# Attention scores with 128 rows in two passes instead of 64 rows in three

## The chip, the cores and the metric

The kernel runs on one core of a Trainium2 chip. The metric is the device time of one execution in microseconds (us). The core has a matrix engine (TensorE, PE in the rows), VectorE (DVE), ScalarE (ACT), GpSimd (POOL) and SyncE (SP), which issues most of the DMA transfers. Matmuls read from the on-chip buffer and write to eight accumulator banks (PSUM), each of 128 partitions by 512 float32 values.

## The reference

Two layers of a transformer block work on 512 image tokens and 256 context tokens of width 1024. Each layer has an adaLN modulation (shift, scale and gate from a 1024 x 6144 matrix), a projection of the tokens, a mixer, an output projection and a SwiGLU. The mixer has three parts: a bidirectional mLSTM of four heads, differential attention of four heads, and grouped-query attention with four query heads over two key heads. The last layer computes no context outputs. What matters here are the attention scores, all with head width 64:

```
p1 = softmax(q1 k1^T / 8),  p2 = softmax(q2 k2^T / 8)     (differential head)
out = (p1 - lam * p2) v
p  = softmax(q k^T / 8),  out = p v                         (grouped-query head)
```

Image queries see all 768 keys, context queries (layer 0 only) the 256 context keys.

## The kernel before, in words

Every float32 product is made from high and low parts. A number is split into a high part, rounded to the matmul type float32r, and the remainder, and a product a b is taken as ah bh + ah bl + al bh (`mm3`). All weights and activations are split this way; for the scores the queries and keys are.

A layer's `mixer` runs in two merged stages. The first holds the mLSTM beside the projections of the output gate, the grouped-query keys, values and queries and the first value heads. The second merges four streams (`merge`, line 354): attention (`att_gqa`, then `att_diff` for heads 0 to 3), the remaining projections (`proj`: queries and keys `b_qk(0)`, `b_qk(1)`, `b_qk(2)`, values, `b_qk(3)`), in layer 0 sixteen steps of the adaLN product (`ada_part`), and the first part of the output projection (`out_first`). `merge` gives the next piece to the stream that is least far by the costs it yields. A planner then orders the instructions of each engine by its own timeline and by these priorities; a tile can be written when one of its pool's buffers (`bufs`) is free.

`b_qk(h)` (line 729) multiplies six token tiles with the weights of a head's queries and keys, rotates them (`do_rope`, line 682), and transposes them on TensorE (`to_feat`, line 719) so that features lie on partitions: the pair's first head on partitions 0 to 63, the second on 64 to 127. `split` (line 413) writes the high part on ScalarE and the low part on VectorE. `b_qk(h)` waits for the scores of an earlier head (`need qkd`) since it takes over its buffers. `b_gkv` and `b_gq` (lines 776 and 794) do the same for the grouped-query heads, with `norm_rope`.

`softmax` (line 813) makes the scores of 128 queries for one or two heads. For each block of 512 keys, and then the remaining 256, it issues three matmuls per head, each with 64 rows of the array:

```
for x, y in ((0, 0), (0, 1), (1, 0)):
    for s, (m, QA, KA, su) in zip(ss, ops):
        hs = slice(64 * m, 64 * m + 64)
        last_qk[key] = mm(s[:, ks], QA[x][hs, qs], KA[y][hs, ks], ...)
```

The result lies in one of two score buffers of two banks each. VectorE takes its minimum (the queries carry a factor of -1/8), ScalarE the exponential with the sum. For four query tiles together, the probabilities are then transposed key block by key block (`transpose_split`), split again (tiles `ph`, `pl`) and multiplied by the values.

The adaLN steps (`ada_part`, line 160) load 128 rows of weights in two transfers of 1024 columns into three buffers (`araw`) and run four matmuls of 512 columns, side by side in four groups of 32 array columns, into the bank `acc`. This is also the only bank for the projections of the second stage. Plain float32 matmuls take two passes, so a step has eight matmul records.

The output projection in `out_first`, `first` and `second` adds to residual tiles `R`; in layer 1 these are first scaled with layer-norm rows (`pgb`) on GpSimd.

Of the kernel before, what the change touches and what calls it, by code (L numbers as in the profile page):

```python
# [12 lines left out]
F32 = mybir.dt.float32  # L13
# [35 lines left out]
def kernel(ctx: ExitStack, tc: tile.TileContext, a: dict, out: bass.AP):  # L49
# [110 lines left out]
    def ada_part(l, sc, ps, ap, tag):  # L160
# [5 lines left out]
        for k in range(KD):  # L166
            raws = []
            for i in range(2):
                raw = ap.tile([P, 1024], F32, tag="araw", name="araw", bufs=3)
                c0 = sc * 2048 + i * 1024  # L170
                nc.sync.dma_start(raw, a["w_ada"][l, k * P:(k + 1) * P, c0:c0 + 1024])
                raws.append(raw)
            pa = ps.tile([P, 512], F32, tag=tag, name="pa")
            for j in range(4):
                TE.matmul(pa[32 * j:32 * j + 32, :], cT[:, k, :], raws[j // 2][:, (j % 2) * 512:(j % 2) * 512 + 512],  # L175
                          start=True, stop=True, tile_position=(0, 32 * j))
            V.tensor_tensor(mod, mod, pa, ALU.add)
            yield 0.9
# [202 lines left out]
    def mixer(l, xh, xl, yd, ps, fill, pre):  # L381
# [300 lines left out]
        def do_rope(dst, src, T, nh):  # L682
# [10 lines left out]
            if dst.ndim == 4:  # L693
                t1, t2 = [t.rearrange("p (v j) d -> p v j d", j=2) for t in (t1, t2)]
            V.tensor_tensor(dst, t1, t2, ALU.add)

        def norm_rope(dst, src, T, nh, gi):
# [8 lines left out]
            if T >= 2:  # L706
                do_rope(dst, t, T, nh)
            else:
                V.tensor_copy(dst, t.rearrange("p (v j) d -> p v j d", j=2) if dst.ndim == 4 else t)

        nqk = 10 if last else 8

        def qk_tile(nm):
            return qkv.tile([P, NTOK], F32R, tag="qk", name=nm, bufs=nqk)
# [4 lines left out]
        def to_feat(rqs, o, dst, ts, after=None, mul=None):  # L719
            pt = ps.tile([P, 512], F32, tag="q", name="ptq")  # L720
            with tc.issue_after(last_qk[after].ins) if after in last_qk else nullcontext():
                for i, rq in enumerate(rqs):
                    TE.transpose(pt[:, i * P:(i + 1) * P], rq[:, o:o + 2].rearrange("p n d -> p (n d)"), ident)
            dh, dl, src = dst[0][:, ts], dst[1][:, ts], pt[:, 0:len(rqs) * P]
            split(dh, dl, src, mul)
# [3 lines left out]
        def b_qk(h, after):  # L729
            def go():  # L730
                wh, wl = wload([cold(C_DQ + h * P, P), cold(C_DK + h * P, P)])
                QA, KA = [qk_tile("QA") for i in range(2)], [qk_tile("KA") for i in range(2)]
                QK[h] = (QA, KA)
                for t0, t1 in ((0, 2), (2, 6)):
# [3 lines left out]
                    for T in range(t0, t1):  # L738
                        po = ps.tile([P, 512], F32, tag="acc", name="po")
                        gemm_b(po[:, c0:256], T, wh, wl, c0, 256 - c0, xh, xl)  # L740
                        rq = qkv.tile([P, 4, HD], F32, tag="rq", name="rq", bufs=4)
                        src = po[:, 0:256].rearrange("p (n d) -> p n d", d=HD)
                        if T >= 2:
                            px = qkv.tile([P, 4, HD], F32, tag="px", name="px", bufs=2)
                            S.copy(px, src)
                            do_rope(rq, px, T, 4)
                        else:
                            S.copy(rq[:, c0 // HD:], src[:, c0 // HD:])
                        rqs.append(rq)
                        yield 2.6  # L750
                    ts = slice(t0 * P, t1 * P)
                    if after is not None:
                        yield ("need", ("qkd", after))
                    if needq:
                        to_feat(rqs, 0, QA, ts, after, -0.125)
                    to_feat(rqs, 2, KA, ts, after)
                    yield 0.3 * (t1 - t0)
# [18 lines left out]
        def b_gkv():  # L776
            wh, wl = wload([cold(C_GK, 256)])
            KG, VG = [qk_tile("KG") for i in range(2)], [v_tile("VG") for j in range(2)]
            for t0, t1 in ((0, 2), (2, 6)):
                rqs = []  # L780
                for T in range(t0, t1):
# [3 lines left out]
                    norm_rope(rq[:, 0:2], po[:, 0:P].rearrange("p (n d) -> p n d", d=HD), T, 2, 1)  # L785
# [4 lines left out]
                to_feat(rqs, 0, KG, slice(t0 * P, t1 * P))  # L790
# [3 lines left out]
        def b_gq():  # L794
            wh, wl = wload([cold(C_GQ, 256)])
            QG = [[qk_tile("QG") for i in range(2)] for j in range(2)]
            for t0, t1 in qgroups:
# [9 lines left out]
                for j in range(2):  # L807
                    to_feat(rqs, 2 * j, QG[j], slice(t0 * P, t1 * P), None, -0.125)
# [4 lines left out]
        def softmax(at, key, T, ops, nk):  # L813
            qs, ss, es = slice(T * P, (T + 1) * P), [], []
# [15 lines left out]
        def hl_tiles(at, n):  # L830
            return [at.tile([P, 512], F32R, tag=t, name=t, bufs=3)[:, 0:n] for t in ("ph", "pl")]
# [12 lines left out]
        def att_diff(at, h):  # L844
            yield ("need", ("qk", h))
            QA, KA = QK[h]
            for t0, t1 in qgroups:
# [26 lines left out]
                sq = at.tile([P, 512], F32, tag="og", name="sq", bufs=3)  # L874
# [3 lines left out]
                else:  # L878
                    ov = at.tile([P, 512], F32, tag="og", name="ov", bufs=3)
# [22 lines left out]
        def att_gqa(at):  # L902
            yield ("need", ("qk", "g"))
            QG, KG, VG = QK["gq"], QK["gk"], VV["g"]
            for t0, t1 in qgroups:
                nk = CTX if t0 == 0 else NTOK
                n = (t1 - t0) * P
                for m in range(2):
                    oG = []
                    for j in range(2):  # L910
# [19 lines left out]
                        og = at.tile([P, 512], F32, tag="og", name="og", bufs=3)  # L930
# [38 lines left out]
        ps.alias = {"q": ("t",)}  # L969
        at = pool("at", bufs=2)  # L970
# [10 lines left out]
        def proj():  # L981
            yield from chain(b_qk(0, None if nqk > 8 else "g"), b_qk(1, "g"), b_qk(2, 0), b_v(2), b_qk(3, 1))
# [6 lines left out]
        def out_first():  # L989
# [15 lines left out]
            for c in range(4):  # L1005
                cs = slice(c * 256, (c + 1) * 256)
                wh, wl = wload([w_out[:, cs]])
                for i in range(2):
                    tg = ("qk", "va")[c % 2]
                    R[c, i] = qkv.tile([P, 3, 256], F32, tag=tg, name="rs", bufs={"qk": nqk, "va": 6}[tg])  # L1010
# [44 lines left out]
        w5 = [[at.tile([P, 512], F32R, tag=t, name="w5", bufs=3) for _ in range(2)] for t in ("ph", "pl")]  # L1055
# [38 lines left out]
        def third(T):  # L1094
            s, g = 1 if T < 2 else 0, T // 2
            if g not in xh:
# [5 lines left out]
                       lambda: at.tile([P, 4, P], F32, tag="og", name="v", bufs=3))  # L1102

        gb1 = [qkv.tile([P, 3, 256], F32, tag="qk", name="gb1", bufs=nqk) for _ in range(3)]
# [52 lines left out]
        at.release()  # L1157
        qkv.release()
# [325 lines left out]
```

## Time and profile before

| | |
|---|---|
| time, median of 3 runs | 2094.97 us (2090.12 to 2097.2) |
| profiled execution, time | 2088.73 us |
| its span, first to last instruction | 2086.8 us |
| TensorE busy | 1957.7 us, 94% |
| VectorE busy | 1132.7 us, 54% |
| ScalarE busy | 748.6 us, 36% |
| GpSimd busy | 332.7 us, 16% |
| mean granted TensorE clock | 0.963 |

Durations of matmuls contain the time until their results are written, so that the records of consecutive matmuls overlap: what one costs in a row of many is the distance between starts. "Busy" is the time covered by at least one record. A timeline row merges neighbours with the same line and tiles, and names the shape of the first; `64*128 64x512` is a stationary tile of 64 rows by 128 columns and a moving tile of 64 rows by 512 columns.

### The profile page before, as it was taken

The numbers are of one execution on the slowest core, as the hardware profiler recorded it, in microseconds if no ns is written. First come the engines' busy times: TensorE is split into PE (matmuls) and PEld (weight loads), VectorE is DVE, ScalarE is ACT, GpSimd is POOL, SyncE is SP. The second block draws the span as 40 slices with busy tenths as digits, with TensorE's granted clock in tenths as the row PEclk, the third lists the DMA queues.
The fourth block names the chain that finished last, engine by engine and source line by source line (L and its number), as shares of the span: only waits on it lengthen the run. The fifth ranks groups of instructions, "written<-read, shape, count | busy, mean of one in ns | idle before, by whom it ended". The sixth has DMA issues, their size and how long they took to land.

```text
span 2086.8 us, 33736 instructions
## 1 busy us (share of the span) xinstructions
PE 1957.7 (94%) x13720; PEld 1753.0 (84%) x13720; DVE 1132.7 (54%) x2247; ACT 748.6 (36%) x1457; POOL 332.7 (16%) x283
## 2 busy tenths in 40 slices
PE   7889899999889999999999988879999889999998
PEld 5778768778879999999987788878888879999886
DVE  3556555666575963532347465845665564232346
ACT  4334364444363111111234333445544352222330
POOL 1224200104316000000000011321016431000000
PEclk9998899999999999999999999989998989999999
DMA  8211261328223772532244521111116215323231
GB/s 289 62 44 36 66 185 38 97 84 226 89 72 102 225 224 63 184 104 62 83 132 149 164 91 31 45 52 41 38 34 173 80 52 172 101 86 98 89 114 61
DMA packets 207221, 215.91 MB, mean 103 GB/s; under 512 B 13584, under 2 KB 181410, under 8 KB 207066
## 3 DMA queue, kind: packets, MB, share of 16 engines
q1 hardware_dynamic: 198778, 205.63, 31.7%
q0 software_dynamic: 8288, 8.13, 1.7%
q8 instruction: 108, 1.77, 0.4%
q14 instruction: 47, 0.39, 0.1%
HBM read 196.12 MB, written 17.60 MB: 102 GB/s over the span
## 4 chain that ended last, share of the span: by engine, by line
PE 80%; DVE 9%; ACT 4%; DMA 3%; issue 2%; POOL 1%; SPq 0%; DVEq 0%; ACTq 0%; POOLq 0%
PE po L63 17%; PE pacc L63 13%; PE pg L63 12%; PE pu L63 12%; PE pc L63 6%; PE s L63 5%; PE pw L63 4%; PE pv L63 3%; PE ppt L837 2%; DVE ca L453 2%; PE pa L175 1%; DMA araw<-w_ada 1%; DVE ru L691 1%; ACT v L271 1%; PE pN L604 1%
## 5 line engine op out<-in xcount | busy, mean ns | idle before, releaser
L63 PE MATMUL po<-wh,xh 128*128 128x256 f32 (+1 forms) x832 | 250.5, 301 | 11.0 <-DVE VG L416 3.5
L63 PE MATMUL po<-wh,xl 128*128 128x256 f32 (+1 forms) x832 | 242.9, 292 | 0.0
L63 PE MATMUL po<-wl,xh 128*128 128x256 f32 (+1 forms) x832 | 242.4, 291 | 0.0
L292 POOL TENSOR_TENSOR wl<-raw,wh 128x1024 fp32r<-128x1024 f32 x56 | 135.9, 2447 | 413.8 <-ACT wh L291 336.9
L291 ACT CAST wh<-raw 128x1024 fp32r<-128x1024 f32 x142 | 142.5, 1048 | 161.7 <-PE pu L63 98.8
L63 PE MATMUL pg<-xh,wh 128*128 128x256 f32 x672 | 190.5, 283 | 1.2 <-ACT v L271 1.2
L63 PE MATMUL pg<-xh,wl 128*128 128x256 f32 x672 | 190.3, 283 | 0.0
L63 PE MATMUL pu<-xh,wh 128*128 128x256 f32 x672 | 190.2, 283 | 0.0
L63 PE MATMUL pu<-xl,wh 128*128 128x256 f32 x672 | 190.2, 283 | 0.0
L63 PE MATMUL pg<-xl,wh 128*128 128x256 f32 x672 | 190.2, 283 | 0.0
L63 PE MATMUL pu<-xh,wl 128*128 128x256 f32 x672 | 190.0, 283 | 0.0
L63 PEld LDWEIGHTS po<-wh,xh 128*128 128x128 f32 x832 | 166.2, 200 | 21.6 <-issue 6.9
L63 PE MATMUL pacc<-wl,hh 128*128 128x512 f32 x440 | 174.2, 396 | 1.0 <-DVE wl L305 1.0
L63 PE MATMUL pacc<-wh,hh 128*128 128x512 f32 x440 | 171.9, 397 | 0.6 <-ACT hh L1293 0.5
L345 POOL TENSOR_TENSOR rstd<-rstd,nhalf 128x4 f32<-128x4 f32 (+2 forms) x52 | 42.9, 830 | 788.1 <-DVE rstd L342 736.5
L63 PEld LDWEIGHTS po<-wl,xh 128*128 128x128 f32 x832 | 166.2, 200 | 1.2 <-issue 0.2
L63 PEld LDWEIGHTS po<-wh,xl 128*128 128x128 f32 x832 | 165.6, 199 | 1.1 <-issue 0.5
L63 PE MATMUL pacc<-wh,hl 128*128 128x512 f32 x440 | 162.5, 397 | 0.0
L1255 DVE SCALAR_TENSOR_TENSOR th<-th,pg 128x512 f32<-128x512 f32 x44 | 30.1, 686 | 208.4 <-ACT th L1254 208.3
L63 PEld LDWEIGHTS pg<-xh,wh 128*128 128x128 f32 x672 | 129.0, 192 | 2.2 <-ACT v L271 1.4
L1254 ACT ACTIVATE th<-pg 128x512 f32<-128x512 f32 x44 | 26.2, 598 | 290.9 <-PE pg L63 279.5
L63 PEld LDWEIGHTS pg<-xh,wl 128*128 128x128 f32 x672 | 129.0, 192 | 0.8 <-issue 0.8
(366 smaller groups left out, 5034.2 us busy)
## 6 DMA issues: line engine op xcount, KB each, us to landing
raw<-w_ffn_in SPq DMA_DIRECT2D x176, 256.0 KB
araw<-w_ada SPq DMA_DIRECT2D x80, 512.0 KB
raw<-w_ffn_out SPq DMA_DIRECT2D x66, 512.0 KB
raw<-w_in SPq DMA_DIRECT2D x32, 512.0 KB
raw<-w_out SPq DMA_DIRECT2D x18, 512.0 KB
araw<-w_ada SPq DMA_DIRECT2D x32, 256.0 KB
raw<-w_in SPq DMA_DIRECT2D x32, 256.0 KB
xr<-x1d SPq DMA_DIRECT2D x10, 512.0 KB
```

The costliest lines, as they stand in the source:

```text
L63: return TE.matmul(out, lhsT, rhs, start=start, stop=stop)
L175: TE.matmul(pa[32 * j:32 * j + 32, :], cT[:, k, :], raws[j // 2][:, (j % 2) * 512:(j % 2) * 512 + 512], start=True, stop=True, tile_positi ...
L271: S.activation(v[:, k], x, AF.Identity, scale=col[:, 0, kk:kk + 1], bias=col[:, 1, kk:kk + 1])
L291: S.copy(h, raw[:, :, 0:n])
L292: wsub[0].tensor_tensor(wl[:, 4 * hf:4 * hf + 4, 0:n], raw[:, :, 0:n], f32(h), op=ALU.subtract)
L345: last_pow[0] = G.tensor_tensor(r, r, nhalf[:, 0:n], op=ALU.pow)
L453: V.scalar_tensor_tensor(ca[:, b0:b0 + n], cr[:, b0 + t:b0 + t + n], cw[:, l, fi, t:t + 1], ca[:, b0:b0 + n], ALU.mult, ALU.add)
L604: TE.matmul(nv[:, j, d, pr], ws[d][:, j, pr], vtok[:, c, 2 * pr + j], start=d + pr == 0, stop=False, skip_group_check=True)
L691: V.tensor_tensor(t2v[:, :, :, bb], sv[:, :, :, 1 - bb], sinb[:, :, bb].unsqueeze(1).to_broadcast([P, nh, 2, 16]), ALU.mult)
L837: TE.transpose(pt[:, i * P:(i + 1) * P], e[:, kt * P:(kt + 1) * P], ident)
L1254: S.activation(th[:, 0:n], gp, AF.Tanh, scale=0.5)
L1255: V.scalar_tensor_tensor(th[:, 0:n], th[:, 0:n], 1.0, gp, ALU.add, ALU.mult)
```

## The change

The queries of one head become one tile of 128 partitions: high part on 64 partitions, low part on the other 64 (`feat_q`). The keys of one head become two tiles of 128 partitions: the high part written on both halves, and the low part on both halves (`feat_k`). A matmul of the query tile with the first key tile gives qh kh + ql kh, with the second qh kl + ql kl. Two matmuls per key block replace three, and the small term ql kl is added. To have keys on both halves, the rotated keys are written twice next to each other (`twice`) and each head of a pair is transposed by itself.

More key tiles need more room: a new pool (`more["pool"]`) holds those of the even heads, and the query tiles of layer 1 shrink to the image tokens. To make room, the tiles `ph`, `pl` and `og` go from three buffers to two, `pgb` from two to one, and the adaLN weights are loaded in four transfers of 512 columns into three buffers of half the size.

```diff
 ada_part:
-            for i in range(2):
-                raw = ap.tile([P, 1024], F32, tag="araw", name="araw", bufs=3)
-                c0 = sc * 2048 + i * 1024
-                nc.sync.dma_start(raw, a["w_ada"][l, k * P:(k + 1) * P, c0:c0 + 1024])
+            for i in range(4):
+                raw = ap.tile([P, 512], F32, tag="araw", name="araw", bufs=3)
+                c0 = sc * 2048 + i * 512
+                nc.sync.dma_start(raw, a["w_ada"][l, k * P:(k + 1) * P, c0:c0 + 512])
...
 do_rope:
-            V.tensor_tensor(dst, t1, t2, ALU.add)
+            for d, n in dst if isinstance(dst, tuple) else ((dst, 0),):
+                u1, u2 = t1[:, n:n + 2], t2[:, n:n + 2]
...
+                elif d.ndim == 4:
+                    u1, u2 = [u.unsqueeze(2).to_broadcast([P, 2, 2, HD]) for u in (u1, u2)]
+                V.tensor_tensor(d, u1, u2, ALU.add)
...
-        nqk = 10 if last else 8
-        def qk_tile(nm):
-            return qkv.tile([P, NTOK], F32R, tag="qk", name=nm, bufs=nqk)
+        def k_tiles(nm, h=1):
+            p = qkv if h % 2 else more["pool"]
+            return [[p.tile([P, NTOK], F32R, tag="qk", name=nm, bufs=4) for _ in range(2)] for _ in range(2)]
+        def q_tiles(nm, h=1):
+            p, n = (qkv, 4) if h % 2 or not last else (more["pool"], 2)
+            return [p.tile([P, NTOK - q0], F32R, tag="qq", name=nm, bufs=n) for _ in range(2)]
...
+        def feat_q(rqs, o, dst, t0, after=None):
+            src = to_feat(rqs, lambda rq: rq[:, o:o + 2].rearrange("p n d -> p (n d)"), after)
+            ts = slice(t0 * P - q0, t0 * P - q0 + len(rqs) * P)
+            for m in range(2):
+                hi, lo = slice(64 * m, 64 * m + 64), slice(64 - 64 * m, 128 - 64 * m)
+                S.mul(dst[m][hi, ts], src[hi], -0.125)
+                V.scalar_tensor_tensor(dst[m][lo, ts], src[hi], -0.125, f32(dst[m][hi, ts]), ALU.mult, ALU.subtract)
+        def twice(rq):
+            return rq.rearrange("p (m u) d -> p m u d", u=2)
+        def feat_k(rqs, dst, t0, after=None):
+            ts = slice(t0 * P, (t0 + len(rqs)) * P)
+            for m in range(2):
+                split(dst[m][0][:, ts], dst[m][1][:, ts],
+                      to_feat(rqs, lambda rq: rq[:, 2 * m:2 * m + 2].rearrange("p n d -> p (n d)"), after))
...
 b_qk:
-                    to_feat(rqs, 2, KA, ts, after)
-                    yield 0.3 * (t1 - t0)
+                    feat_k([rq[1] for rq in rqs], KA, t0, after)
+                    yield 0.4 * (t1 - t0)
...
 softmax:
-            for k0 in range(0, nk, 512):
-                ks = slice(k0, min(nk, k0 + 512))
-                for x, y in ((0, 0), (0, 1), (1, 0)):
-                    for s, (m, QA, KA, su) in zip(ss, ops):
-                        hs = slice(64 * m, 64 * m + 64)
-                        last_qk[key] = mm(s[:, ks], QA[x][hs, qs], KA[y][hs, ks], x + y == 0, x == 1)
+            for s, (m, QA, KA, su) in zip(ss, ops):
+                for k0 in range(0, nk, 512):
+                    ks = slice(k0, min(nk, k0 + 512))
+                    for i in range(2):
+                        last_qk[key] = mm(s[:, ks], QA[m][:, qs], KA[m][i][:, ks], i == 0, i == 1)
...
-            return [at.tile([P, 512], F32R, tag=t, name=t, bufs=3)[:, 0:n] for t in ("ph", "pl")]
+            return [at.tile([P, 512], F32R, tag=t, name=t, bufs=2)[:, 0:n] for t in ("ph", "pl")]
...
-                    pgb = rp.tile([P, 2, 256], F32, tag="pgb", name="pgb", bufs=2)
+                    pgb = rp.tile([P, 2, 256], F32, tag="pgb", name="pgb", bufs=1)
```

## Rows read from the trace of the kernel before

**Rows 1.** The page: span, and TensorE's busy time, share and instructions.

```profile
span 2086.8 us, 33736 instructions
...
PE 1957.7 (94%) x13720; PEld 1753.0 (84%) x13720; DVE 1132.7 (54%) x2247; ACT 748.6 (36%) x1457; POOL 332.7 (16%) x283
```

**Rows 2.** Stretches: length; busy us of PE, PEld, DVE, ACT, POOL; clock; DMA.

```profile
238.00:345.00 107.00, 103.49 (x644) 79.44 (x642) 50.03 (x108) 57.42 (x127) 10.17 (x5) 0.97 0.39 121
345.00:560.00 215.00, 206.77 (x1445) 173.53 (x1445) 138.60 (x306) 91.72 (x208) 40.66 (x31) 0.98 0.39 115
...
1380.00:1465.00 85.00, 83.28 (x577) 72.84 (x576) 41.19 (x83) 44.62 (x87) 9.61 (x4) 1.00 0.13 37
1465.00:1600.00 135.00, 132.11 (x870) 114.35 (x869) 85.46 (x161) 63.83 (x131) 27.79 (x19) 0.96 0.23 68
1600.00:1700.00 100.00, 81.87 (x516) 71.97 (x516) 64.20 (x120) 39.69 (x76) 45.67 (x31) 0.83 0.35 97
```

**Rows 3.** Stretches, only what writes or reads the score tile (no POOL).

```profile
1600.00:1640.00 40.00, 12.25 (x48) 9.00 (x48) 7.43 (x8) 7.87 (x16) 0.79 0.38 98
sum 600.00, PE 131.57 PEld 94.65 DVE 100.55 ACT 105.87; mean PE 26.31 PEld 18.93 DVE 20.11 ACT 21.17
```

**Rows 4.** The score tile's instructions: ns min/median/max, first and last start, shapes.

```profile
L63 PE MATMUL s<-KA,QA x432: 271/383/792, 348.4 to 1623.1; 64*128 64x256 f32 x80, 64*128 64x512 f32 x64
...
L63 PE MATMUL s<-KG,QG x216: 271/366/502, 220.2 to 1463.0; 64*128 64x512 f32 x64, 64*128 64x256 f32 x44
L824 DVE TENSOR_REDUCE mx<-s x120: 398/950/959, 220.9 to 1624.7; 128x1 f32<-128x768 f32 x96, 128x1 f32<-128x256 f32 x24
```

**Rows 5.** Timeline of TensorE around one score product: start us, length us, what.

```profile
357.06 0.28 PE L63 MATMUL po<-wl,xh 128*128 128x256 f32 x1
357.18 0.28 PE L63 MATMUL po<-wh,xl 128*128 128x256 f32 x1
357.39 1.32 PE L63 MATMUL s<-KA,QA 64*128 64x512 f32 x6
358.64 0.39 PE L63 MATMUL po<-wh,xh 128*128 128x256 f32 x1
358.86 0.28 PE L63 MATMUL po<-wl,xh 128*128 128x256 f32 x1
```

**Rows 6.** Timeline of TensorE: first, a paired, and the last run of scores.

```profile
220.21 0.50 PE L63 MATMUL s<-KG,QG 64*128 64x256 f32 x2
...
555.90 1.33 PE L63 MATMUL s<-KA,QA 64*128 64x512 f32 x12
557.16 0.39 PE L63 MATMUL pw<-wh,xh 128*128 128x256 f32 x1
...
1611.50 3.31 PE L63 MATMUL s<-KA,QA 64*128 64x512 f32 x12
```

**Rows 7.** The chain that ended last, one piece: start us, us, what.

```profile
1955.27 123.19 PE pacc L63 x525
```

**Rows 8.** Timeline of TensorE: four transposes.

```profile
413.20 0.60 PE L837 MATMUL ppt<-ident,e 128*128 128x128 f32 x4
```

**Rows 9.** Timeline of TensorE: adaLN bursts, the first, one between, the last.

```profile
271.94 1.06 PE L175 MATMUL pa<-araw,cT 128*32 128x512 f32 x8
...
297.81 1.05 PE L175 MATMUL pa<-araw,cT 128*32 128x512 f32 x4
...
491.08 1.07 PE L175 MATMUL pa<-araw,cT 128*32 128x512 f32 x8
```

**Rows 10.** The chain that ended last: one adaLN load.

```profile
290.80 4.66 DMA araw<-w_ada
```

**Rows 11.** Groups by line: count, busy us, mean ns, idle before (VectorE, ScalarE).

```profile
L419 DVE SCALAR_TENSOR_TENSOR QA<-ptq,QA 128x512 fp32r<-128x512 f32 x3 | 2.1, 691 | 1.4 <-ACT QA L418 1.4
...
L695 DVE TENSOR_TENSOR rq<-rt,ru 128x256 f32<-128x256 f32 x14 | 5.9, 420 | 0.5
...
L418 ACT ACTIVATE QA<-ptq 128x512 fp32r<-128x512 f32 x4 | 2.4, 600 | 2.4 <-PE ptq L723 2.4
```

More of the change, by code (lines that the diff above doesn't have):

```diff
@@ L174, in ada_part @@
             for j in range(4):
-                TE.matmul(pa[32 * j:32 * j + 32, :], cT[:, k, :], raws[j // 2][:, (j % 2) * 512:(j % 2) * 512 + 512],
+                TE.matmul(pa[32 * j:32 * j + 32, :], cT[:, k, :], raws[j],
                           start=True, stop=True, tile_position=(0, 32 * j))
@@ L731, in go @@
                 wh, wl = wload([cold(C_DQ + h * P, P), cold(C_DK + h * P, P)])
-                QA, KA = [qk_tile("QA") for i in range(2)], [qk_tile("KA") for i in range(2)]
+                QA, KA = q_tiles("QA", h), k_tiles("KA", h)
                 QK[h] = (QA, KA)
@@ L754, in go @@
                     if needq:
-                        to_feat(rqs, 0, QA, ts, after, -0.125)
-                    to_feat(rqs, 2, KA, ts, after)
-                    yield 0.3 * (t1 - t0)
+                        feat_q([rq[0] for rq in rqs], 0, QA, t0, after)
+                    feat_k([rq[1] for rq in rqs], KA, t0, after)
+                    yield 0.4 * (t1 - t0)
                 yield ("done", ("qk", h))
@@ L777, in b_gkv @@
             wh, wl = wload([cold(C_GK, 256)])
-            KG, VG = [qk_tile("KG") for i in range(2)], [v_tile("VG") for j in range(2)]
+            KG, VG = k_tiles("KG"), [v_tile("VG") for j in range(2)]
             for t0, t1 in ((0, 2), (2, 6)):
@@ L795, in b_gq @@
             wh, wl = wload([cold(C_GQ, 256)])
-            QG = [[qk_tile("QG") for i in range(2)] for j in range(2)]
+            QG = [q_tiles("QG") for j in range(2)]
             for t0, t1 in qgroups:
@@ L969, in mixer @@
         ps.alias = {"q": ("t",)}
+        more["pool"] = pool("qkw", bufs=1, side="right")
         at = pool("at", bufs=2)
@@ L981, in proj @@
         def proj():
-            yield from chain(b_qk(0, None if nqk > 8 else "g"), b_qk(1, "g"), b_qk(2, 0), b_v(2), b_qk(3, 1))
+            yield from chain(b_qk(0, None if last else "g"), b_qk(1, "g"), b_qk(2, 0), b_v(2), b_qk(3, 1))
             yield ("done", "proj")
@@ L1054, in mixer @@
         fa = FfnA(l)
-        w5 = [[at.tile([P, 512], F32R, tag=t, name="w5", bufs=3) for _ in range(2)] for t in ("ph", "pl")]
+        w5 = [[at.tile([P, 512], F32R, tag=t, name="w5", bufs=2) for _ in range(2)] for t in ("ph", "pl")]
         raw = wp.tile([P, DM], F32, tag="raw", name="raw", bufs=3)
@@ L1101, in third @@
                        cols[(l, "ffn", s)], two["tx"],
-                       lambda: at.tile([P, 4, P], F32, tag="og", name="v", bufs=3))
-        gb1 = [qkv.tile([P, 3, 256], F32, tag="qk", name="gb1", bufs=nqk) for _ in range(3)]
+                       lambda: at.tile([P, 4, P], F32, tag="og", name="v", bufs=2))
+        gb1 = [qkv.tile([P, 3, 256], F32, tag="qk", name="gb1", bufs=4) for _ in range(3)]
         for i in range(8):
@@ L1157, in mixer @@
         at.release()
+        more["pool"].release()
         qkv.release()
```

45 lines of the change are left out of this document (25 added, 20 removed).

## The prediction

> **What bounds the kernel now.** I read the page first: TensorE is busy for 94% of a span of 2086.8 us [rows 1]. Then I cut the span into stages. The scores are computed in the attention stretch of each layer, about 238 to 560 us and 1380 to 1640 us. Up to 560 us in layer 0 and up to 1600 us in layer 1 TensorE is busy for 96 to 98% and VectorE for 47 to 64% [rows 2]: what TensorE gets rid of there shortens the stretch, as long as something else is ready. From 1600 to 1700 us it is busy for 82% at a granted clock of 0.83; that stretch is a chain through several engines, and less TensorE work there is worth little. Score matmuls take 131.57 us of TensorE in all, 12.25 of it after 1600 us [rows 3].
>
> **Scores.** Today there are 432 + 216 = 648 score matmuls for 120 products, 96 over 768 keys and 24 over 256 [rows 4]. A 768-key product is six: three of 512 columns, three of 256. A timeline row names the shape of its first one only. One product alone starts at 357.39 and the next projection matmul at 358.64: 1.25 us [rows 5]. The neighbours pay as well. Projection matmuls otherwise start 0.12 us apart (357.06, 357.18). The last one before the scores is followed after 0.21, and the first one after them after 0.22. So a run costs some 0.19 us more than its own 1.25: 1.44. These are the changes between 64-row and 128-row matmuls.
>
> The new product is two passes of 128 rows, four matmuls. Their price is that of the other 128-row matmuls with this type: 512 columns 123.19/525 = 0.235 us [rows 7], 256 columns 0.12. Per 768-key product 0.71, per 256-key product 0.24, with no change of rows. The trace has no such score matmul; from both sides, the cheap end is half of the pitch, 0.36 per 768-key product, if two heads' passes could overlap as two 64-row ones can, and the dear end is today's 64-row price, 1.25 for six, that is 0.83 for four. I take the pitches: matmuls of the same shape that follow each other. The ends move the sum by -40 and +15.
>
> The sum: a run's record ends 0.07 us after its follower starts (357.39 + 1.32 against 358.64). I count 107 runs in the timeline, 64 in layer 0 and 43 in layer 1; the first and the last are in [rows 6]. Before: 131.6 - 107 x 0.07 + 107 x 0.19 = 144.4. After: 96 x 0.71 + 24 x 0.24 = 73.9, and 3 more for the half-speed stretch of the last head. Some ten runs touch an adaLN burst, which changes the array's shape anyway: 2 less. Saved: 144.4 - 73.9 - 3 - 2 = 65 us, about half of it in each layer.
>
> A rule speaks against this. Where the two heads of a differential pair stand side by side, they do run together: the run at 555.90 holds twelve matmuls, two products, and takes 1.26 us, no more than one alone [rows 6]. The Trainium skill ("TensorE: Matmul & The Clock Gate", Part 3: Packing small matmuls) says that matmuls in different row groups run concurrently, starting some 4 ns apart; by it alone the differential heads would save next to nothing. The trace agrees for that run, 1.26 + 0.19 for a pair against 2 x 0.71. But 120 products come in 107 runs, so most runs hold one product alone, and the measured total of the sum above has the pairing that does happen in it.
>
> **Keys and queries.** Each key group is transposed twice, once per head, with the token's key written twice. Per layer that is 6 more transposes for each of four heads and for the grouped-query keys: 60 in all, at (0.60 - 0.27)/3 = 0.11 us [rows 8], 0.27 being one with its drain: 6.6 us of TensorE. On ScalarE and VectorE every split of queries or keys becomes two of the same length, half as tall for queries. At 0.60 and 0.69 us for 512 columns [rows 11], scaled to some 0.37 and 0.41 for 256, a differential head of layer 0 gets 1.9 us of ScalarE and 2.2 of VectorE more, and the second rope addition at up to 0.42 us adds four times that. A half-tall split could cost from half of these to the full price; I take the full one. Layer 0 gains at most 20 us of VectorE, layer 1 some 15. TensorE hides them: VectorE is at 65% in 345 to 560 us [rows 2] and would be near 75%. Uncovered, they sit in front of a head's first scores, some 2 us each, 16 us over eight heads.
>
> **adaLN loads in layer 0.** Sixteen steps form the modulation, four matmuls each. Now two loads of 512 KB feed a step, out of three buffers; after it is four loads of 256 KB, still out of three buffers, so the fourth can be issued only when the first matmul of its own step has read its buffer. The price per burst on TensorE doesn't depend on how many of the four run in it: the bursts with all passes (x8) take 1.06 and 1.07 us, one with half of them (x4) takes 1.05 [rows 9]. There are 21 bursts now, first and last shown, for 16 steps. A step can no longer be one burst: at least 32, at most 64 when each load is awaited singly. Between 280 and 310 us, where the loads set the pace (the chain holds one for 4.66 us [rows 10]), singles are likely; in the later steps three and one. I take 42, that is 21 more at 0.98 + 0.19 for the changes of shape: 25 us, between 13 and 50.
>
> **Smaller edits, costed at nothing.** Pairs of probability tiles and output tiles go from three buffers to two: other heads' projections fill TensorE meanwhile; uncovered, a cast and a subtraction (0.60 + 0.69 us) per key block. The layer-norm rows of layer 1 go from two buffers to one, so a load waits on SP for GpSimd, with the next weight loads behind it; these rows are needed only for the last columns of the output product, past 1640 us; without that cover three loads at up to 4.66 us, 14 us. New tiles in the freed region and the reassigned slots wait for the same heads as before. Together I put 4 us for waits.
>
> **Sum.** TensorE: -65 + 6.6 + 25 = -33. Of the savings some 4 us fall after 1600 us, where TensorE isn't the bound, and 4 us come back as waits: -25. The profiled execution took 2088.7 us (span 2086.8 and 1.9 around it), so it would take about 2064. The median of the runs shown, 2095.0, lies 6.2 above it: I forecast 2070.
>
> **Rivals.**
> - The adaLN steps stall (slower). A step's output bank is also the only bank of the projections, so while the fourth load is on its way no projection can start. If nothing else is ready, a step loses the load: about 3.9 us, an estimate under the 4.66 of the load twice as large. Sixteen of these are 62, and the result is 2070 + 62 = 2132; with half covered 2101. It decides from 25/16 = 1.6 us uncovered per step. For it: the steps run while queries and keys of the next heads wait for the grouped-query scores. Against it: softmax, transposes and value products fill TensorE to 97% there today.
> - The softmax chain becomes the bound. A product needs its maximum and exponential before the score bank is free, and VectorE's share nears 75%. If 40% of the scores' gain turns into waits, 26 come back: 2096, no change. For it: after 1600 us, with the projections gone, TensorE falls to 82%; against it: before that it is full.
> - The adaLN bursts stay in groups (32) and nothing waits: 12 + 4 us less, 2054.
> - Pairing is worth more than I count: where two products of a differential head stand together, 1.45 us become 1.42 [rows 6], 1 us over 32 pairs. The grouped-query heads would still save 32 x 0.73, and some 0.5 on each of 8 short products, 27 in all: -27 + 6.6 + 25 + 4 = +9, 2104. The measured total of the score rows speaks against it. This is the rule of the Trainium skill named above.
>
> **How the numbers follow.** Forecast 0.55 (its own range 2052 to 2086), adaLN stall 0.14, softmax chain 0.14, groups 0.14, pairing 0.03. Eight in ten: from 2040 (the groups case with a part of the cheap end of the score passes) to 2108 (the stall half covered, or the dear end of several terms). A difference under 0.3%, 6 us, can't be told from none. Faster: 0.53 of the forecast, 0.14 of the groups, 0.03 of the softmax case: 0.70. Slower: stall and pairing with 0.01 of the softmax case: 0.18. The same: 0.12.
>
> **What would show it.** 432 score matmuls of 128x512 and 128x256, with starts 0.235 and 0.12 us apart and no 0.2 us step beside them; score time on TensorE near 80 us; 60 more transposes; 35 to 50 adaLN bursts, of x2 to x6. Both attention stretches shorter, layer 1's more, by 20 to 28 us, layer 0's by 0 to 10. Wrong if score matmuls cost more than their pitch, if layer 0 grows with waits for the modulation loads, or if TensorE's share falls below 90% in stretches where it is now 97%.

## The result, and the profile after

The changed kernel takes 2116.88 us (median of 4 runs, 2113.4 to 2119.34) against 2093.76 of the kernel before: ratio 1.0109, 95% interval 1.0086 to 1.0133, some 23 us slower. The forecast was 2070, 25 below the 2095.0 that it started from. Differences below are ratios to the kernel before times 2092 us; an interval of 0.002 to either side is 4 us.

The page after, answering [rows 1]: TensorE has 13 us less to do, and the span is 25 us longer.

```profile
span 2111.6 us, 33665 instructions
...
PE 1944.9 (92%) x13564; PEld 1740.6 (82%) x13564; DVE 1155.7 (55%) x2316; ACT 769.8 (36%) x1502; POOL 335.5 (16%) x287
```

The score tile's instructions after, answering [rows 4]: 432 matmuls of 128 rows instead of 648 of 64.

```profile
L63 PE MATMUL s<-KA,QA x288: 274/364/799, 353.2 to 1657.5; 128*128 128x256 f32 x80, 128*128 128x512 f32 x64
...
L63 PE MATMUL s<-KG,QG x144: 274/285/796, 222.9 to 1492.3; 128*128 128x256 f32 x80, 128*128 128x512 f32 x64
```

The timeline of TensorE after, around one product between projection matmuls, answering [rows 5]: the product starts 0.12 us after its neighbour and the next matmul follows 0.69 after its start, then 0.12 again. This lone run costs 0.69 where one cost 1.44, as forecast; over all runs of four score matmuls the median is 0.80.

```profile
1425.05 0.28 PE L63 MATMUL po<-wh,xl 128*128 128x256 f32 x1
1425.17 0.86 PE L63 MATMUL s<-KG,QG 128*128 128x512 f32 x4
1425.86 0.28 PE L63 MATMUL po<-wh,xh 128*128 128x256 f32 x1
1425.98 0.28 PE L63 MATMUL po<-wl,xh 128*128 128x256 f32 x1
```

Stretches after, columns as in [rows 2]. Layer 1's stretches start 31 us later, since layer 0 is that much longer. TensorE's busy share fell from 96 to 89% in 345 to 590, from 98 to 94% in the first stretch of layer 1 and from 98 to 91% in the second, and the granted clock from 1.00 and 0.96 to 0.94.

```profile
238.00:345.00 107.00, 100.76 (x568) 69.88 (x569) 49.01 (x111) 57.82 (x130) 5.92 (x4) 0.97 0.36 109
345.00:590.00 245.00, 217.44 (x1455) 179.44 (x1454) 154.16 (x339) 105.34 (x236) 57.57 (x42) 0.97 0.38 114
1411.00:1496.00 85.00, 80.26 (x578) 74.51 (x578) 46.43 (x99) 47.71 (x94) 9.57 (x4) 0.94 0.20 55
1496.00:1631.00 135.00, 123.49 (x822) 110.52 (x820) 95.83 (x177) 67.88 (x139) 39.06 (x29) 0.94 0.23 65
1631.00:1731.00 100.00, 84.82 (x561) 76.60 (x562) 64.12 (x137) 45.20 (x89) 39.14 (x27) 0.86 0.36 101
```

One adaLN step after, in the timeline of TensorE (the bracket is the idle time before, and its releaser), answering [rows 9]. Each matmul leaves two records: x6 are three of the step's four, and the fourth, whose load had to wait for a buffer, comes 5 us later in a burst of its own.

```profile
490.82 1.06 PE L175 MATMUL pa<-araw,cT 128*32 128x512 f32 x6
...
496.01 1.05 PE L175 MATMUL pa<-araw,cT 128*32 128x512 f32 x2 [1.84 <-DMA araw<-w_ada]
```

TensorE's busy time on these matmuls, in three windows from 238 to 560 us (only the sum is shown), is 22.24 us before in 21 bursts; after, in 42 bursts (two of them take 1.9 us, at the lower clock), it is:

```profile
sum 322.00, PE 45.80; mean PE 15.27
```

By stage, the last output matmul of layer 0 starts at 664.3 us instead of 633.4, the whole of the loss and more; from there to the first score of layer 1 nothing changes (748.7 and 748.8 us), and from that score to the start of the last output matmul layer 1 takes 312.0 instead of 318.7. The forecast had layer 1 shorter by 20 to 28 us and layer 0 by 0 to 10.

### The profile page after: what moved, and what is told of

The parts are those of the page before. It is cut to its first block, busy times and chain, and to the rows that moved or that the text cites. A ratio compares the mean times of both kernels' runs of the same rounds, so it can differ in the third digit from the quotient of the medians.

```text
span 2111.6 us, 33665 instructions
## 1 busy us (share of the span) xinstructions
PE 1944.9 (92%) x13564; PEld 1740.6 (82%) x13564; DVE 1155.7 (55%) x2316; ACT 769.8 (36%) x1502; POOL 335.5 (16%) x287
## 4 chain that ended last, share of the span: by engine, by line
PE 78%; DVE 12%; ACT 5%; issue 2%; DMA 2%; POOL 1%; DVEq 0%; SPq 0%; ACTq 0%; POOLq 0%
PE po L63 16%; PE pacc L63 14%; PE pu L63 12%; PE pg L63 12%; PE pc L63 6%; PE pw L63 5%; PE s L63 3%; PE pv L63 2%; DVE ca L453 2%; PE ppt L866 2%; PE pa L175 2%; DMA araw<-w_ada 1%; ACT v L271 1%; DVE mx L853 1%; DVE ru L691 1%
```

## The experiments

All ran after the forecast. Theory A at the start: the adaLN steps, cut into four loads, are the loss. Rival: the smaller buffers. Both assumed that the scores had brought what was forecast; that fell in the second set.

**The adaLN loads.** b_ada3 puts only the four loads into the kernel before; b_ada6 does so with six buffers; a_ada4 gives the changed kernel a fourth buffer.

```
b_ada3, b_ada6 (before)           a_ada4 (after)
-for i in range(2):               -name="araw", bufs=3
-  raw = [P, 1024], bufs=3        +name="araw", bufs=4
+for i in range(4):               -rt, gsq, px: bufs=2
+  raw = [P, 512], bufs=3 (or 6)  +bufs=2 if last else 1
```

> The kernel before with only the adaLN part of the change: four loads of 256 KB per step into three buffers of half the size. Theory A (the adaLN loads cost layer 0 what the scores gave): 25 to 40 us slower than before, with some 40 adaLN bursts instead of 21 and the projections of the second stage late. Theory B (the loss comes from the other buffers cut from three to two, or from the doubled keys): within 8 us of before.

> The kernel before with four adaLN loads of 256 KB per step, but into six buffers, the same room as before. It separates the size of a load from the number of buffers. Theory A, in the form that the fourth load of a step waits for its first matmul: within 8 us of before, with 16 to 30 bursts. If the smaller loads themselves were slow: 15 us or more slower.

> The changed kernel with four adaLN buffers instead of three, so that a whole step can be loaded ahead; the room comes from the projection copy and the rotation product with one buffer instead of two in layer 0. Theory A: 25 to 40 us faster than the changed kernel, 2077 to 2092, some 16 to 24 adaLN bursts. Theory B: it stays above 2105.

Measured: b_ada3 2126.3, ratio 1.0164 [1.0140, 1.0188], +34 us; b_ada6 2098.26, 1.0036 [1.0022, 1.0050], +7.5; a_ada4 2116.53, 1.0121 [1.0103, 1.0138], no better than the changed kernel. So the split loads cost 34 us by themselves, with enough buffers 7.5, and yet a fourth buffer mends nothing. b_ada3 has 39 bursts, b_ada6 26 and a_ada4 31; the busy time of b_ada6 and of a_ada4 on them, same windows:

```profile
sum 322.00, PE 27.44; mean PE 9.15
```

```profile
sum 322.00, PE 35.13; mean PE 11.71
```

Then one load per step for all four matmuls, in both kernels, which takes the loads' rate and the wait in mid-step away:

```
-for i in range(4): ... dma_start(raw, w_ada[..., c0:c0 + 512]); raws.append(raw)
+dma_start(raw, w_ada[..., sc * 2048:sc * 2048 + 512]); raws = [raw] * 4
```

> The kernel before, with only one 256 KB modulation load per step instead of two of 512 KB, its tile used by all four matmuls of the step (three quarters of w_ada is not read, so the modulation values are not the reference's). It is the reference for the same edit in the kernel after: it says what the modulation loads cost where they were cheapest. Theory A (the modulation steps of the kernel before already cost little): 2075 to 2085, 6 to 16 us below the 2091 of the kernel before, since 8.8 us of its 21 runs were waits for a load or starts of a second burst. Theory B (the steps are hidden in it): 2089 to 2093.

> The kernel after, with one 256 KB modulation load per step for all four matmuls (the same three quarters of w_ada left out). No step can wait for its own first matmul any more; everything else of the change stays. Theory A (the four loads over three buffers are the cause of the loss: 34 us of it when made alone in the kernel before): 34 to 44 us below the kernel after, 2073 to 2083, and the attention of layer 0 ends as early as in the kernel before. Theory B (a second cause of the same stage, the doubled key transposes and the smaller buffers, takes over once the first is gone, as the run with four buffers suggests): no more than 15 us below the kernel after, 2100 to 2112.

Measured: b_one 2087.67, 0.9988 [0.9967, 1.0009]; a_one 2089.73, 0.9977 [0.9954, 1.0000]. Theory B held for b_one (2.5 us won, not 6 to 16). a_one is 27.6 us below the changed kernel: well over theory B's 15, though short of the 34 that theory A wanted. TensorE's busy time on the 16 bursts of a_one:

```profile
sum 322.00, PE 17.05; mean PE 5.68
```

That is 28.75 us less than after, for 27.6 us of time. The two traces show in which form it went: in layer 0, from the first score to the last output matmul, after (first row) is 27 us longer than a_one (second row); TensorE is busy 24 us more in it and idle only 3 us more.

```profile
222.90:664.70 441.80, 384.67 (x2451) 308.63 (x2450) 268.00 (x611) 204.37 (x450) 82.59 (x62) 0.95 0.35 103
```

```profile
226.30:641.10 414.80, 360.49 (x2451) 310.56 (x2450) 270.99 (x611) 204.13 (x450) 81.88 (x62) 0.92 0.27 79
```

But the other half of this pair is the surprise: with cheap adaLN steps the changed kernel is no faster than the kernel before with the same steps (0.9977 and 0.9988). All the rest of the change, the shorter scores among it, is together worth nothing beyond the errors.

What was left of a_ada4: a_px1 makes only the single buffers that gave it room, and a_half cuts each step into two half steps, so that none has to wait for a load that its own matmul must first make room for.

```
a_half: for each k, for i in range(2): two loads, pa, two matmuls,
        V.tensor_tensor(mod[64 * i:64 * i + 64], ..., ALU.add); yield 0.45
a_px1:  rt, gsq, px: bufs=2 if last else 1
```

> The kernel after with every modulation step cut into two half steps: two 256 KB loads, an output bank, two matmuls and one addition each, so that with three buffers no half step waits for a load that its own matmul must first make room for, and one load is always ahead. The same values are computed. There are then 32 or a few more bursts instead of 43. Theory A (the loss of the four loads is the wait in mid-step, with the projections' bank held): 15 to 25 us below the kernel after, 2090 to 2102. Theory B (it is the number of bursts, about 1 us each however few matmuls run in one): 8 to 12 below, 2103 to 2109. Theory C (it is the loads' own rate with a single one ahead): within 5 us of the kernel after.

> The kernel after with the rope's input and scratch tiles of layer 0 in single buffers (px, rt, gsq: 1 instead of 2), the modulation loads left at three buffers: the part of the run with four load buffers that was made only to find room. Theory A (these single buffers cost what the fourth buffer won, so that run hid a gain): 2127 to 2145, 10 to 28 us above the kernel after, since each projection's copy then waits for the rope before it. Theory B (they cost nothing, and a fourth load buffer is worth nothing): 2113 to 2121.

Measured: a_half 2112.05, 1.0088 [1.0062, 1.0115], 4 us below the changed kernel; a_px1 2120.99, 1.0137 [1.0115, 1.0160], 6 above. Measured as 2121 us a_px1 lies at the upper end of theory B, and against the changed kernel between the two: the single buffers hid some 6 us of a_ada4, with an interval that reaches none. a_half won almost nothing, as its theory C had it; but its loads came in singly, so that it has 42 bursts, not the 32 that I expected, and as much time on TensorE as after:

```profile
sum 322.00, PE 47.81; mean PE 15.94
```

Nor did it take the wait in mid-step away. From the first matmul of a step to the end of the addition that reads it, the projections' only bank is taken; in the traces this sums to 47 us before, 109 after, 92 in a_half and 30 in a_one. So a_half doesn't settle whether that wait is the loss. Over all these kernels a burst takes 1.06 to 1.14 us (22.24/21, 27.44/26, 35.13/31, 45.80/42, 17.05/16, 47.81/42). The time rises with the number of bursts, but not one for one, and with an exception: b_ada3 spends 21.75 us more on them than before and is 34 slower, while a_ada4 spends 10.7 less than the changed kernel and is no faster, and its single buffers explain only some 6 of that. The bank is taken for less time in a_ada4 too (66 us), so neither count explains that run. That the four loads over three buffers are the loss is shown; how a burst becomes time is shown only for after against a_one, where it is TensorE's busy time.

**The smaller buffers.** b_bufs makes only these in the kernel before; b_og2 only those of the attention outputs.

```
b_bufs: ph, pl, w5, og (sq, ov, og, v): bufs=3 -> 2; pgb: bufs=2 -> 1
b_og2:  og (sq, ov, og, v): bufs=3 -> 2
```

> The kernel before with only the smaller buffer counts: probability and output tiles with two buffers instead of three, layer-norm rows with one instead of two. Theory A: within 6 us of before. Theory B: 15 to 30 us slower.

> The kernel before with two buffers instead of three for the attention outputs alone (og: the evicted value products, their squares and the layer-norm tiles that share them). All the smaller buffers together cost 8.7 us. Theory A (og is that cost, as in layer 1 of the mixed version, where a third buffer won 6 us): 5 to 10 us above the kernel before. Theory B (it is the probability tiles, and og is covered in the kernel before): within 3 us of it.

Measured: b_bufs 2100.0, 1.0038 [1.0021, 1.0055], +8 us; b_og2 2097.28, 1.0025 [1.0001, 1.0050], +5. The larger part seems to be the attention outputs' buffers, as theory A of b_og2 has it, at its lower end; the two intervals overlap.

**The doubled keys.** a_one_k1 is a_one with only the first head's keys transposed and split (two short copies stand in for the others; the keys are still written twice by the rope).

```
-for m in range(2): split(dst[m][0]..., to_feat(...))
+for m in range(1): split(dst[m][0]..., to_feat(...))
-mm(s[:, ks], QA[m][:, qs], KA[m][i][:, ks], ...)
+mm(s[:, ks], QA[m][:, qs], KA[0][i][:, ks], ...)
```

> The kernel after with one modulation load per step, and only the first head's keys of each pair transposed and split, used for both heads (the second head's keys are left out, and three quarters of w_ada). It takes away the 60 extra transposes and the key splits that the change doubled. Theory A (the doubled keys cost what the forecast put on TensorE, 7 us, and hide on the other engines): 2080 to 2085, 5 to 10 us below the same kernel with both heads' keys (2089.7). Theory B (their waits cost more, key split before transpose bank before scores): 2070 to 2079. Theory C (hidden): 2088 to 2091.

Measured: 2072.57, 0.9922 [0.9899, 0.9944]: 11.5 us below a_one, uncertain by 7, slightly over theory A; the time as such lies in theory B's range. In the traces nearly all of it is in layer 1: from the first score to the last output matmul that takes 298 us instead of 313, layer 0 414 instead of 415.

**What score time is worth.** b_two leaves the third pass out of the kernel before; b_two_y also lowers the planned cost of a product, by which the order is written out; a_one_three puts a third 128-row pass into a_one.

```
b_two:       -for x, y in ((0, 0), (0, 1), (1, 0)):  +for x, y in ((0, 0), (0, 1)):
b_two_y:     -yield 1.94, 0.97 * nk / NTOK           +yield 1.3, 0.65 * nk / NTOK
a_one_three: -for i in range(2): KA[m][i]            +for i in range(3): KA[m][i // 2]
```

> The kernel before with the third pass of every score product (low query by high key) left out: two 64-row passes of the same tiles, nothing else changed, no buffer, load or transpose. It takes away a third of the 144 us of score occupancy, 48 us, and asks what shorter scores alone are worth. Theory A (TensorE bounds the stage, the forecast's reading): 2043 to 2060, 31 to 48 us below the kernel before. Theory B (where TensorE is freed of score time, the chain of softmax, eviction and split is next, and the order of work is fixed by planned costs): 2075 to 2088, 3 to 16 us below, and TensorE's idle time grows by 30 us or more.

> The kernel before with two score passes, and the planned cost of a product lowered by the same third (1.94 to 1.3 and 0.97 to 0.65), by which the order of the instructions is written out. Theory A (the order still plans for three passes, so other heads' projections come at the wrong places and TensorE waits): 2065 to 2078. Theory B (the order matters little; waits and clock move elsewhere): 2080 to 2090.

> The kernel after with one modulation load per step (three quarters of w_ada left out) and a third 128-row pass put back into every score product (the high keys twice, so that the attention weights are not the reference's). At the pitches seen in the kernel after, 0.355 us per 768-key product and 0.12 per short one, that is 37 us more of TensorE in the attention stretches, with every other part as it is. It prices score time in the changed kernel itself. Theory A (a microsecond of score time is worth a quarter to a half there, the rest is covered by the chain and by TensorE's waits): 8 to 18 us above the same kernel with two passes, ratio to the kernel before 1.001 to 1.007. Theory B (it is worth its full length): 30 to 40 above, ratio 1.012 to 1.017.

Measured: b_two 2084.44, 0.9947 [0.9929, 0.9965]: 11 us for a third of the score passes, theory B. The forecast's 48 us was too much for them, since the steps beside each run stay: counted from each score matmul's start to the next start, waits left out, score time falls by 30 us, from 124 to 94. b_two_y 2086.28, 0.9982 [0.9969, 0.9996]: 7 us worse than b_two, so the old planned cost isn't what holds the gain back. a_one_three 2110.66, 1.0115 [1.0072, 1.0158]: 29 us above a_one, between the theories and nearer to B; its four runs lie apart (2103.68 to 2119.16), and the two profiled executions differ by 13.5 (2103.68 and 2090.20). By starts it has 36 us more of score time than a_one. Within that spread it gives no exact price, but one nearer to its full length than to a half.

Where it goes is seen in layer 1, from the first score to the last projection matmul, a stretch without adaLN. The rows are, one kernel each: before, b_two, after, a_one_three, a_one_k1 (columns as in [rows 2]).

```profile
1382.20:1597.50 215.30, 210.98 (x1413) 183.15 (x1412) 125.40 (x239) 106.31 (x215) 35.35 (x20) 0.98 0.18 54
```

```profile
1381.10:1597.60 216.50, 209.45 (x1299) 181.78 (x1299) 120.34 (x237) 105.04 (x213) 35.37 (x20) 0.89 0.17 48
```

```profile
1413.00:1624.40 211.40, 196.99 (x1361) 179.72 (x1360) 135.40 (x265) 111.55 (x225) 42.47 (x26) 0.94 0.21 58
```

```profile
1396.90:1613.40 216.50, 205.09 (x1454) 187.36 (x1453) 141.52 (x267) 112.95 (x227) 43.59 (x28) 0.97 0.20 58
```

```profile
1386.00:1589.00 203.00, 187.42 (x1323) 170.89 (x1322) 133.35 (x261) 107.42 (x218) 50.09 (x30) 0.96 0.23 63
```

b_two has 114 matmuls fewer than before and is busy as long, at a granted clock of 0.89 instead of 0.98: the stretch isn't shorter at all. After, TensorE is busy 14 us less, the stretch is 4 shorter, and 10 us more are idle. By starts, the scores give up 16 us there and the matmuls beside them 8; 3 go to the added transposes and 8 to the other matmuls, 0.136 us each on average where it was 0.131, at a granted clock of 0.94 instead of 0.98. a_one has the same numbers there as after (211.40 us, 197.01 busy, 1361 matmuls); in a_one_three 93 matmuls more take 8 us more of TensorE and 5 of time, at a higher clock. Freed score time becomes idle time and time at the lower clock, and the reverse. Without the second head's keys the stretch gives 8 us.

**The chain.** A short row maximum takes 0.55 us of VectorE from each long product, between scores and exponential, in the kernel before, in b_two and in a_one.

```
-V.tensor_reduce(mx, s[:, 0:nk], AX.X, ALU.min)
+V.tensor_reduce(mx, s[:, 0:CTX], AX.X, ALU.min)     (queries times -0.0125, was -0.125)
```

> The kernel before, with the row maximum of the scores taken over the first 256 keys only (and the scores scaled by a tenth, so that the exponential stays finite; the attention weights are not the reference's). It shortens VectorE's part between scores and exponential from 0.95 to 0.40 us for 96 products, 53 us of VectorE, and touches no matmul. Theory A (in the kernel before TensorE bounds the attention stretch): 2087 to 2093, no gain. Theory B (the chain score, maximum, exponential, transpose already sets the pace): 2065 to 2080.

> The kernel before with two score passes (the third left out) and the short maximum of the run beside it. If the chain of softmax took over where TensorE got free, the short maximum must be worth more here than in the kernel with three passes. Theory A (chain bound after the cut): 2060 to 2074, at least 10 us below the two-pass kernel's 2084, and at least 10 below the run with the short maximum alone. Theory B (what was won on TensorE goes into its lower clock and a fixed order of work, not into waits for the maximum): 2080 to 2086, within 5 us of two passes alone.

> The kernel after with one modulation load per step (three quarters of w_ada left out) and the row maximum over the first 256 keys only (scores scaled by a tenth): the short maximum in the kernel with two 128-row passes. Theory A (behind the shorter scores the chain of maximum, exponential and split sets the pace, as in the kernel with two of three passes, where the short maximum was worth 9 us): 9 to 20 us below the same kernel with the full maximum, ratio to the kernel before 0.988 to 0.993. Theory B (the doubled keys and smaller buffers set it): within 4 us, ratio 0.996 to 1.000.

Measured: b_mx 2082.85, 0.9976 [0.9959, 0.9994]; b_two_mx 2070.28, 0.9904 [0.9879, 0.9929]; a_one_mx 2075.22, 0.9914 [0.9890, 0.9938]. The same cut is worth 5 us in the kernel before, 9 behind two 64-row passes and 13 behind two 128-row passes. The order is theory A's: the shorter the scores, the more the chain behind them counts. With intervals of 4 to 5 us on each number the middle step isn't shown by itself; 5 against 13 is hardly more than their errors.

**A mixture.** hybrid has layer 0's mixer and adaLN loads of the kernel before and layer 1's mixer of the changed one; hybrid_og3 gives the latter its third og buffer back, for which layer 1 has room.

```
mixer(l) = three-pass mixer if l == 0 else two-pass mixer; ada_part of before
hybrid_og3: og (sq, ov, og, v) in layer 1: bufs=2 -> 3
```

> Layer 0's mixer and the modulation steps as in the kernel before, layer 1's mixer as in the kernel after: the two-pass scores where no modulation loads run beside them. From the stages of the two traces: layer 0 keeps the time of before, and layer 1 is 7 to 11 us shorter (first score to last output product 318.7 before, 312.0 after). Theory A: 2080 to 2086, 5 to 11 us below the kernel before. Theory B (layer 1's gain came from what layer 0's delay had let arrive early): 2090 to 2095, no gain.

> Layer 0's mixer and modulation as in the kernel before, layer 1's mixer as in the kernel after but with three buffers for the attention outputs (og) instead of two. It asks whether the change pays where its room allows the old buffers. Theory A (the smaller buffers took a part of layer 1's gain): 2078 to 2084 against 2090 of the kernel before, 3 to 8 us below the version with two. Theory B (the buffer is covered in layer 1): the same as the version with two, ratio to the kernel before 0.997 to 1.000.

Measured: hybrid 2089.97, 0.9988 [0.9967, 1.0009], no gain; hybrid_og3 2083.86, 0.9960 [0.9945, 0.9974], 8 us faster than the kernel before and 31 faster than the changed one. So the change pays in layer 1. That the one buffer decides it is not shown: the two differ by 6 us with an interval of some 5, and in the profiled executions layer 1 takes 314 us from the first score to the last output matmul in both, against 319 before; they differ outside that stage.

## Why the prediction was wrong

As ratios times 2092 us, the parts come out so. The adaLN steps: after against a_one, less before against b_one, 27.6 - 2.5 = 25. The smaller buffers: 8. The doubled keys: 11.5. The scores by what is left: a_one stands 2 us below b_one, so the scores brought 2 - (- 8 - 11.5), that is 21.5 us. The sum 25 + 8 + 11.5 - 21.5 = 23 is the loss, by construction; each part is uncertain by some 5 us or more, so the scores' by some 10; the buffers were priced in the other kernel, and what no run took out alone (the queries' halves, the second rope addition, the moved tiles) stands in the scores' part.

- **The step that failed is the scores' 65 us, taken as time one for one.** The 432 matmuls without a step beside them came as said, and so did the 20 us of the neighbours: against others of their kind, the matmuls beside the runs took 9 to 11 us too long in layer 0 and 9 in layer 1 before, and about nothing after. Two things were wrong. The sum was too large: counting every score matmul from its start to the next start, waits left out, score time goes from 124 to 90 us, not to 77, since a run of four takes 0.80 us in the median, not 0.71, its first matmul 0.31 and not 0.235, and the clock is lower. So some 53 instead of 65. (The cheap end of the passes would be 36 us by the forecast's own prices, not 40.) And of these 53 only about 21 became time. The forecast read a share of 97% as "what TensorE gets rid of shortens the stretch". In layer 1's stretch it got rid of 14 us net and the stretch lost 4; b_two, with nothing else changed, won 11 of 30.
- **Waits of 4 us** (and "as long as something else is ready"): this is where a part of the rest went. TensorE's idle time between the first score and the last output matmul grew from 32 to 57 us in layer 0 and from 23 to 31 in layer 1; b_bufs alone has 42 in layer 0, so some of it is the buffers', and some of the rest is the lower clock. The second rival, the softmax chain, for which I took 2096 and 40% of the gain, comes nearest: some 60% of the gain did not become time, and the short maximum points to that chain without proving it. I had held the full share of before against it, which says only what is full as long as the scores are long.
- **adaLN, 25 us for 42 bursts:** right in number (42) and size (25; 34 when made alone). The first rival had the sign of the result, but not its form: TensorE's own waits for a load are small, as the waits' row after shows (total, times, longest), against 1.0 before, and against a_one TensorE idles 3 us more in layer 0, not 62. While a step holds the projections' bank, other work does run.

```profile
PE pa L175 <- DMA araw<-w_ada: 8.8, 8, 3.2
```

- **Keys, 6.6 us:** 11.5. "TensorE hides them" failed in part, if the 5 us between them are more than error. The splits were priced rightly (of the differential heads' keys, 16 casts and 16 subtractions became 32 of each, at medians of 0.49 and 0.55 us). The second rope addition takes 0.72 us for a key written twice, not 0.42, as the group of it in a_one shows; but a_one_k1 has it too, so it is no part of the 11.5, and which wait makes them up stays open.

```profile
L697 DVE TENSOR_TENSOR rq<-rt,ru 128x256 f32<-128x256 f32 x17 | 12.3, 723 | 0.2 <-PE ptq L733 0.2
```

- **Smaller buffers "costed at nothing":** 8 us, some 5 of them og. "Other heads' projections fill TensorE meanwhile" was wrong in part. The layer-norm rows, priced at 14 us uncovered, were not run alone; with the probability tiles they make up the other 3.
- **Pairing.** The fourth rival had the right sign too (2104). The Trainium skill's rule ("TensorE: Matmul & The Clock Gate", Part 3: Packing small matmuls), that matmuls in different row groups run at the same time, agrees with the pairs: the shortest run of twelve matmuls takes 1.26 us [rows 6], the shortest of eight after it 1.39, no gain; the median of the thirteen runs of twelve in the differential heads takes 1.83 us, so it holds in part. By this rival the differential heads save next to nothing, and TensorE's busy time on their scores fell by 16 us (before, then after), since most runs held one product. So this is not the cause.

```profile
sum 755.00, PE 85.18; mean PE 42.59
```

```profile
sum 755.00, PE 69.52; mean PE 34.76
```

"Wrong if TensorE's share falls below 90% in stretches where it is now 97%" was the right sign to watch: 89% in 345 to 590 us and 91% in layer 1's second stretch. The other two signs came as well: score matmuls cost more than their pitch, and layer 0 grew, though hardly by waits for the loads.

What stays open is why a burst's microsecond cost a full one between a_one and after, and a score's less than a half: 11 of 30 in b_two, about 21 of 53 by what is left. a_one_three speaks against a fixed price, with 29 us, uncertain by 10, for 36 put back. Scores begin a chain that must run through VectorE and ScalarE in any case, and bursts are pure extra work; that fits, but no run tested it.

## What to carry over

A busy share of 97% is a state of the order as it is, not a proof that the engine is the bound: before pricing a cut one for one, cut the same work out roughly (one pass left out) and see what it brings; here that run would have said a quarter of the 48 us that the forecast's prices give for the pass. Price the room that a change needs like its arithmetic: the buffers and loads that were made smaller cost 33 us against the 21 that the scores brought. And apply a change only in the stage that has room for it: in layer 1 alone, with one buffer back, it won 8 us.

## What the hardware showed unexpectedly

The granted clock fell where score passes were taken out: before it stayed at 1.00 from 1460 to 1490 us, and in b_two, with a third of the score passes gone, it was 0.80 and 0.75 there (windows of b_two; the clock is the third column from the right). These are means: by the trace TensorE ran at the lower of its two levels, 1.2 GHz, from 1469.0 to 1482.6 us and at 2.4 GHz around that.

```profile
1430.00:1445.00 15.00, 13.84 (x102) 12.14 (x100) 5.40 (x12) 8.44 (x17) 4.85 (x2) 1.00 0.26 71
1445.00:1460.00 15.00, 15.00 (x107) 13.13 (x106) 8.29 (x21) 7.55 (x15) 0.00 (x0) 1.00 0.10 36
1460.00:1475.00 15.00, 13.95 (x77) 11.64 (x76) 9.55 (x19) 10.47 (x20) 4.72 (x2) 0.80 0.24 70
1475.00:1490.00 15.00, 15.00 (x81) 12.90 (x81) 5.87 (x12) 4.37 (x9) 0.00 (x0) 0.75 0.01 2
```

The second row of low clock is fully busy with 81 matmuls; the row with 107 at full clock is as busy. So here TensorE took back a part of what was cut from it by running slower, and the busy share doesn't show it; the clock's column does. A gap alone doesn't tell when it falls: 13.28 busy us in 1430 to 1445 of the kernel before were followed by 1.00.

And a burst of adaLN matmuls at full clock takes 1.04 to 1.07 us whether one, two or four run in it (x2, x4, x8).
